# A 31-tap depthwise convolution as matrices of 4 time phases x 32 channels on TensorE

## The chip, the cores and the metric

The kernel runs on one core of a Trainium2 chip. The metric is the device time of one execution in microseconds (us); lower is better. A core has TensorE (matrix products, written to PSUM), VectorE, ScalarE (activations and casts), GpSimd and SyncE, whose only work here is to issue DMAs. In the lines of the profile they are PE (PEld for its weight loads), DVE, ACT, POOL and SP. "L165" is line 165 of the kernel file.

## What is computed

A trunk of four layers over 512 tokens of 1024 channels in float32. Each layer has a token mixer and then a gated conv-FFN, both behind an RMS norm and with a residual sum. The mixers are, in order: conv module, neighbourhood attention, retention, conv module. The change is inside the conv module, which so runs twice, as the first and the fourth mixer:

```python
def dwconv(x, w, b):
    k, c = w.shape
    y = lax.conv_general_dilated(
        x, w[:, None, :].astype(x.dtype), window_strides=(1,),
        padding=[(k // 2, k // 2)], dimension_numbers=('NWC', 'WIO', 'NWC'),
        feature_group_count=c)
    return y + b

def conv_module(h, w_in, b_in, dw_w, dw_b, ln_g, ln_b, w_out):
    a, gt = jnp.split(h @ w_in + b_in, 2, axis=-1)
    u = a * jax.nn.sigmoid(gt)
    u = dwconv(u, dw_w, dw_b)
    u = layernorm(u, ln_g, ln_b)
    return jax.nn.silu(u) @ w_out
```

`dw_w` has 31 taps per channel, so every output of the depthwise convolution is a weighted sum of 31 neighbouring tokens of its own channel.

## The kernel before

**Layout and arithmetic.** Activations lie channel-major: a tile is 128 channels (partitions) by 512 tokens, and `x` is eight such tiles. Matrix products run in the format `F32R`. To keep float32 accuracy each operand is split into a high part (a cast to `F32R` on ScalarE) and a low part (the difference, on VectorE), and `mm3` issues three matmuls per product: high x high, high x low, low x high. Weights come as tiles of 128 x 1024 on SyncE's DMA queue (`load_raw`, L150) and are split by `split_w` (L159 on ScalarE, L160 on VectorE). `split` (L174, L175) does the same for activations. The lines of `mm3` are L164 to L166.

**Order.** The program is written with a scheduler that orders the instructions of each engine from their order in the source, their readiness in its own model of time, and free buffers. On the chip every engine then runs its queue in that fixed order and waits for what is missing. `tc.issue_after` adds an order by hand. A pool with `bufs=n` has n buffers for a name; a tile that finds none free waits for the oldest to be read.

**The conv stage, `conv`.** It walks over m = 0..7, the groups of 128 channels.

- `front(m)`: the in-projection of value and gate, 2 x 24 matmuls of 512 columns into two PSUM banks; the norm's factor is applied afterwards (L341, L343), sigmoid on ScalarE (L342), the product is `u` (L345), padded by 15 zeros on either side. Then `u` is split into `uh`, `ul`, and the first taps run on TensorE: per tap a 128 x 128 diagonal matrix of the tap's weights, high and low, multiplied with `u` shifted by the tap, into bank `A`. How many taps go there stands in `TAPS`: the first number of each triple, for each layer and group. The diagonal matrices are built by `diag`, on GpSimd (L370) or ScalarE (L375).
- `taps(m, u, A)`, called two groups later (`LT`): the second number of taps goes as a product on ScalarE (L387, L391) and a sum on GpSimd (L392, into `pacc`); the others go on VectorE, partly into `A` (L406), partly into the tile `c8[m]` (L398, L402, L409). L411 and L412 add the three.
- `lnstat(m)`, two groups after that (`LS`): four transposes on TensorE (L420) and statistics per token on VectorE (L422), because the layer norm runs over channels.
- After the loop the statistics are combined, mean and `rstd` are spread over partitions by transposes (`bcast`, L200), and per group VectorE subtracts and multiplies (L460, L463), ScalarE applies Silu and the cast (L464, L466) and VectorE makes the low part (L469). Then eight outputs of the out-projection, 24 matmuls each, are added to `x` (`residual`, L244) and handed on to the next stage's `prep`.

For the first layer the weights of group 0 are loaded and split ahead, in the program's last part, together with `x`.

Of the kernel before, what the change touches and what calls it, by code (L numbers as in the profile page):

```python
# [8 lines left out]
F32 = mybir.dt.float32  # L9
# [8 lines left out]
P = 128  # L18
T = 512
# [14 lines left out]
for _name, _w in (  # L34
    ("n1g", 32), ("n2g", 32), ("cbin", 32), ("cdw", 2 * 8 * CW), ("cdb", 16),
    ("clg", 16), ("clb", 16), ("qg", 1), ("kg", 1), ("gng", 16), ("logd", 8),
    ("fdw", 4 * 44 * FC), ("fdb", 4 * 44),
):
    COLS[_name] = _n
    _n += _w  # L40
# [8 lines left out]
ID = True  # L49
# [7 lines left out]
NDB = 3  # L57
NPB = 0
NU = 3
NPR = 4  # L60
LT = 2
LS = 2
DH = ("PPPAPPPP", "PPPPPPPP")
DL = ("AAAAAAAP", "AAAAPAAP")
# [13 lines left out]
def tile_trunk(  # L78
# [3 lines left out]
    cw_in, cw_out, nat_qkv, rpb, nat_out,  # L82
# [220 lines left out]
    def conv(j, after):  # L303
        PAD = CW // 2
        TW = T + 2 * PAD
        dw0 = COLS["cdw"] + j * 8 * CW
        with ExitStack() as st:
            stage_pools(st, 9, 4, 4)
            cp = st.enter_context(tc.tile_pool(name=nm("cv"), bufs=1, reuse_waits=RW))
            c8 = [cp.tile([P, T], F32, tag=f"c{i}", name=nm("c")) for i in range(8)]  # L310
            bst = cp.tile([P, 4, 8, 6], F32, tag="bst", name=nm("bst"))
            dwh = cp.tile([P, 8 * CW], F32R, tag="dwh", name=nm("dwh"))
            dwl = cp.tile([P, 8 * CW], F32, tag="dwl", name=nm("dwl"))
            with ExitStack() as s2:
                up = s2.enter_context(tc.tile_pool(name=nm("cvu"), bufs=1, reuse_waits=RW))
                dp = s2.enter_context(tc.tile_pool(name=nm("cvd"), bufs=2, reuse_waits=RW))
                rp = s2.enter_context(tc.tile_pool(name=nm("cvr"), bufs=NPR, reuse_waits=RW))
                us = [up.tile([P, TW], F32, tag=f"u{i}", name=nm("u")) for i in range(NU)]
                for u in us:
                    nc.vector.memset(u[:, :PAD], 0.0)  # L320
                    nc.vector.memset(u[:, PAD + T:], 0.0)
                def front(m):
# [9 lines left out]
                    else:  # L332
                        for (ps, c) in ((pa, m), (pg, m + 8)):
                            wh, wl = load_w(cw_in[j, c], D)
                            for k in range(KD):
                                s = slice(k * P, (k + 1) * P)
                                mm3(ps, wh[:, s], wl[:, s], xhi[k], xlo[k], k == 0, k == KD - 1)
                            if m == 0:
                                stats1() if c == 0 else stats2()
# [8 lines left out]
                    npe = TAPS[j][m][0]  # L348
                    if ID and m not in diags:
                        with tc.issue_after(state["sqlast"].ins):  # L350
                            diags[m] = diag(m)
                    dh, dl = diags.pop(m) if m in diags else diag(m)
                    uh = dp.tile([P, TW], F32R, tag="uh", name=nm("uh"))
                    ul = dp.tile([P, TW], F32R, tag="ul", name=nm("ul"))
                    split(u, uh, ul)
                    for i in range(npe):
                        mm3(A, dh[:, i, :], dl[:, i, :], uh[:, i:i + T], ul[:, i:i + T],
                            i == 0, i == npe - 1)
                    return m, u, A

                diags = {}

                def diag(m):
                    npe = TAPS[j][m][0]
                    dh = dp.tile([P, npe, P], F32R, tag="dh" if m < 7 else "dh7", name=nm("dh"), bufs=NDB if m < 7 else 1)
                    dl = dp.tile([P, npe, P], F32R, tag="dl" if m < 7 else "dl7", name=nm("dl"), bufs=NDB if m < 7 else 1)
                    idb = ident.unsqueeze(1).broadcast_to([P, npe, P])
                    for dst, src, eng in ((dh, dwh.bitcast(F32), DH[j][m]), (dl, dwl, DL[j][m])):
                        if eng == "P":
                            nc.gpsimd.tensor_tensor(  # L370
                                dst, idb,
                                src[:, m * CW:m * CW + npe].unsqueeze(2).broadcast_to([P, npe, P]), MUL)
                        else:
                            for i in range(npe):
                                nc.scalar.activation(dst[:, i, :], ident, AF.Copy,  # L375
                                                     scale=src[:, m * CW + i:m * CW + i + 1])
                    return dh, dl

                def taps(m, u, A):
                    npe, npool, na = TAPS[j][m]  # L380

                    def wt(tap):
                        c = dw0 + m * CW + tap
                        return pt[:, c:c + 1]

                    pacc = dp.tile([P, T], F32, tag="pacc", name=nm("pacc"))
                    nc.scalar.activation(pacc, u[:, npe:npe + T], AF.Identity,  # L387
                                         bias=pc("cdb", j * 8 + m), scale=wt(npe))
                    for tap in range(npe + 1, npe + npool):
                        pr = rp.tile([P, T], F32, tag="pr", name=nm("pr"))  # L390
                        nc.scalar.activation(pr, u[:, tap:tap + T], AF.Copy, scale=wt(tap))  # L391
                        nc.gpsimd.tensor_tensor(pacc, pacc, pr, ADD)  # L392
                    ta = list(range(npe + npool, npe + npool + na))
                    tb = list(range(npe + npool + na, CW))
                    B = c8[m]
                    if tb:
                        t = tb.pop(0)
                        nc.vector.tensor_scalar(B, u[:, t:t + T], wt(t), None, MUL)  # L398
                    lead = max(0, len(tb) - len(ta))
                    for n in range(lead):  # L400
                        t = tb.pop(0)
                        nc.vector.scalar_tensor_tensor(B, u[:, t:t + T], wt(t), B, MUL, ADD)  # L402
                    while ta or tb:
                        if ta:
                            t = ta.pop(0)
                            nc.vector.scalar_tensor_tensor(A, u[:, t:t + T], wt(t), A, MUL, ADD)  # L406
                        if tb:
                            t = tb.pop(0)
                            nc.vector.scalar_tensor_tensor(B, u[:, t:t + T], wt(t), B, MUL, ADD)  # L409
                    if npe + npool + na < CW:  # L410
# [5 lines left out]
                def lnstat(m):  # L416
# [4 lines left out]
                    for b in range(4):  # L421
                        nc.vector.bn_stats(bst[:, b, m, :], tp[:, b * P:(b + 1) * P])  # L422
# [654 lines left out]
```

## Time and profile before

| | us |
|---|---|
| median of 3 runs | 2710.16 |
| lowest and highest run | 2708.76, 2711.47 |
| profiled execution, span | 2709.2 |
| busy in it: TensorE | 2583.4 |
| VectorE | 1824.4 |
| ScalarE | 1115.2 |
| GpSimd | 493.6 |

The span runs from the first to the last instruction of one profiled execution; engines work side by side, so the busy times don't add up to it. The DMAs moved 232.01 MB. The first conv stage fills the first 269 us of the span, the fourth mixer lies between about 2077 and 2335 us. Most of the rest is in-projections, FFNs and attention on TensorE.

A group line of the profile gives line, engine, operation, output and inputs, shape and count; then the busy time of the group in us and the mean of one in ns; then the engine's idle time ahead of it and what ended it. A timeline line gives start and duration in us. A line of waits gives who waited for whom, the total in us, how often, and the longest. Where matmuls overlap, their durations are longer than the distance of their starts.

### The profile page before, as it was taken

What the parts mean: (1) busy time and instruction counts of PE and PEld (TensorE: products, weight loads), DVE (VectorE), ACT (ScalarE), POOL (GpSimd) and SP (SyncE); (2) the same over time, 40 slices, a digit from 0 to 9 for tenths busy, and PEclk for the clock granted to TensorE, in tenths of its full rate; (3) what the DMA queues carried; (4) which work ended last, traced back from release to release, by engine and by line L of the source; (5) the groups of instructions that cost most, each with busy time, mean ns of one, the idle gap of its engine ahead of it and who ended that gap; (6) DMA issues with size and microseconds to landing.
All of it is one profiled execution on the core that took longest, in us unless ns stands there. A gap on an engine that the chain in (4) does not pass through costs nothing.

```text
span 2709.2 us, 31043 instructions
## 1 busy us (share of the span) xinstructions
PE 2583.4 (95%) x12018; PEld 2108.1 (78%) x12018; DVE 1824.4 (67%) x2742; ACT 1115.2 (41%) x1628; POOL 493.6 (18%) x337
## 2 busy tenths in 40 slices
PE   7878999999999999999999999999999776999999
PEld 5656888889998788888888888788887664888887
DVE  8997677535888777734656466777634999677732
ACT  6544444333655444423333323444423544444421
POOL 5873000002432100000000000100002874200000
PEclk9888999999999999999999999999999897999999
DMA  3111422333333222233222221222232110322232
GB/s 119 47 39 55 146 93 94 95 94 105 98 93 93 78 94 94 90 93 112 78 86 70 86 76 64 87 94 94 92 98 89 48 39 23 102 94 93 93 104 84
DMA packets 72995, 232.01 MB, mean 86 GB/s; under 512 B 11920, under 2 KB 16144, under 8 KB 72848
## 3 DMA queue, kind: packets, MB, share of 16 engines
q1 hardware_dynamic: 71488, 225.48, 26.2%
q0 software_dynamic: 640, 3.15, 0.5%
q8 instruction: 94, 1.54, 0.2%
q10 hardware_dynamic: 720, 1.41, 0.2%
q14 instruction: 53, 0.43, 0.1%
HBM read 224.50 MB, written 5.63 MB: 85 GB/s over the span
## 4 chain that ended last, share of the span: by engine, by line
PE 83%; DVE 15%; issue 1%; ACT 1%; DMA 0%; SPq 0%; ACTq 0%; DVEq 0%
PE ps L165 25%; PE ps L164 25%; PE ps L166 24%; DVE c L402 4%; PE ps L170 3%; PE ps L171 3%; PE ps L169 3%; DVE c L409 2%; DVE wl L160 2%; DVE ps L406 1%; DVE c L411 1%; DVE u L345 1%; DVE xl L214 1%; DVE ul L175 1%; DVE bst L422 0%
## 5 line engine op out<-in xcount | busy, mean ns | idle before, releaser
L159 ACT CAST wh<-wr 128x1024 fp32r<-128x1024 f32 (+1 forms) x414 | 427.1, 1032 | 1049.7 <-PE ps L165 789.6
L165 PE MATMUL ps<-xl,wh 128*128 128x512 f32 x1920 | 768.6, 400 | 4.3 <-DVE xl L214 4.3
L164 PE MATMUL ps<-xh,wh 128*128 128x512 f32 x1920 | 762.5, 398 | 8.8 <-ACT xh L213 6.7
L166 PE MATMUL ps<-xh,wl 128*128 128x512 f32 x1920 | 761.9, 397 | 3.6 <-DVE wl L160 3.6
L160 DVE TENSOR_TENSOR wl<-wr,wh 128x1024 fp32r<-128x1024 f32 (+1 forms) x410 | 514.2, 1255 | 341.8 <-ACT wh L159 339.3
L164 PEld LDWEIGHTS ps<-xh,wh 128*128 128x128 f32 x1920 | 363.8, 189 | 101.3 <-ACT xh L213 7.7
L165 PEld LDWEIGHTS ps<-xl,wh 128*128 128x128 f32 x1920 | 363.8, 189 | 92.3 <-DVE xl L214 6.6
L166 PEld LDWEIGHTS ps<-xh,wl 128*128 128x128 f32 x1920 | 363.8, 189 | 90.6 <-DVE wl L160 4.4
L222 POOL TENSOR_TENSOR sqacc<-t,sqacc 128x512 f32<-128x512 f32 x49 | 78.8, 1608 | 1188.4 <-ACT t L220 1168.6
L166 PE MATMUL ps<-hh,wl 128*128 128x512 f32 x704 | 278.0, 395 | 0.0
L164 PE MATMUL ps<-hh,wh 128*128 128x512 f32 x704 | 278.0, 395 | 0.0
L165 PE MATMUL ps<-hl,wh 128*128 128x512 f32 x704 | 278.0, 395 | 0.0
L392 POOL TENSOR_TENSOR pacc<-pacc,pr 128x512 f32<-128x512 f32 x155 | 255.3, 1657 | 77.0 <-ACT pr L391 58.9
L268 DVE TENSOR_TENSOR t<-ps,rstd_bc 128x512 f32<-128x512 f32 x176 | 120.9, 691 | 157.6 <-PE ps L166 157.3
L244 DVE TENSOR_TENSOR x<-ps,x 128x512 f32<-128x512 f32 x80 | 54.7, 690 | 170.3 <-PE ps L166 170.3
L170 PE MATMUL ps<-wl,xh 128*128 128x256 f32 (+1 forms) x512 | 159.2, 312 | 0.6 <-DVE wl L160 0.6
L171 PE MATMUL ps<-wh,xl 128*128 128x256 f32 (+1 forms) x512 | 159.1, 312 | 0.0
L169 PE MATMUL ps<-wh,xh 128*128 128x256 f32 (+1 forms) x512 | 158.5, 312 | 0.0
L166 PEld LDWEIGHTS ps<-hh,wl 128*128 128x128 f32 x704 | 132.3, 188 | 31.9
L165 PEld LDWEIGHTS ps<-hl,wh 128*128 128x128 f32 x704 | 132.3, 188 | 31.8
L164 PEld LDWEIGHTS ps<-hh,wh 128*128 128x128 f32 x704 | 132.3, 188 | 31.7
L271 ACT ACTIVATE t<-t,par 128x512 f32<-128x512 f32 x176 | 142.7, 815 | 11.8 <-DVE t L268 11.7
(222 smaller groups left out, 3609.8 us busy)
## 6 DMA issues: line engine op xcount, KB each, us to landing
wr<-in_f_up SPq DMA_DIRECT2D x176, 512.0 KB, 3.5
wr<-in_f_down SPq DMA_DIRECT2D x64, 448.0 KB, 3.4
wr<-in_f_down SPq DMA_DIRECT2D x32, 512.0 KB, 3.5
wr<-in_cw_in SPq DMA_DIRECT2D x30, 512.0 KB, 3.4
wr<-in_nat_qkv SPq DMA_DIRECT2D x24, 512.0 KB, 3.6
wr<-in_cw_out SPq DMA_DIRECT2D x16, 512.0 KB, 3.4
wr<-in_ret_qk SPq DMA_DIRECT2D x16, 512.0 KB, 3.4
wr<-in_ret_v SPq DMA_DIRECT2D x16, 512.0 KB, 3.4
```

The costliest lines, as they stand in the source:

```text
L159: nc.scalar.copy(hi[:, :n], raw[:, :n])
L160: eng.tensor_tensor(lo[:, :n], raw[:, :n], hi[:, :n].bitcast(F32), SUB)
L164: nc.tensor.matmul(o, wh, ah, start=first, stop=False)
L165: nc.tensor.matmul(o, wh, al, start=False, stop=False)
L166: nc.tensor.matmul(o, wl, ah, start=False, stop=last)
L169: nc.tensor.matmul(o, ah, wh, start=first, stop=False)
L170: nc.tensor.matmul(o, ah, wl, start=False, stop=False)
L171: nc.tensor.matmul(o, al, wh, start=False, stop=last)
L268: nc.vector.tensor_tensor(u, ps, rstd_bc, MUL)
L271: nc.scalar.activation(a, u, AF.Identity, bias=pc("fdb", l * 44 + c), scale=pt[:, w + 1:w + 2])
L392: nc.gpsimd.tensor_tensor(pacc, pacc, pr, ADD)
L402: nc.vector.scalar_tensor_tensor(B, u[:, t:t + T], wt(t), B, MUL, ADD)
```

## The change

All 31 taps run on TensorE, without diagonal matrices. The time axis is cut into four phases (token = 4q + s, `SH` = 4) and the channels into blocks of 32, so a contraction over 128 partitions holds 4 phases x 32 channels. For each block of 32 channels a matrix of 128 x 128 maps the four input phases to the four output phases at one shift of q, and nine shifts (`NA`) cover the 31 taps. The host prepares these matrices (`cdw`): 32 blocks per layer, each 128 x 1152 float32, 0.590 MB.

- `front(m)` computes the gate before the value, writes `u` phase by phase with four zeros at either end of each (`QL` = 136), splits it into `hl`, writes `hl` to DRAM with one DMA from GpSimd's queue and reads it back with four, rearranged to `X`: partitions 4 phases x 32 channels, for four blocks.
- `taps(m, X)`, two groups later (`LAG`): per block the raw matrices are loaded on SyncE's queue and split. For each of nine shifts `X` is the stationary operand: one matmul of 256 columns (X high by the matrix's high and low) and one of 128 columns (X low by the high part). The result comes out token-major: partition q, columns phase and channel. Two VectorE instructions of 256 columns per half group add the products, the bias and write it to `y`.
- The layer norm's statistics are then along the free axis (three `bn_stats` per phase); mean and `rstd` are per-partition scalars. `norm(k)` normalises four pieces of 128 columns, transposes them back to channel-major on TensorE, and ScalarE applies Silu; then the split as before.
- The out-projection's first two outputs advance together with `norm`, chunk by chunk. Tokens are in the order phase, q, so the residual sum (`finish`) reads PSUM and writes `x` through a rearranged view.
- The vector and GpSimd taps, the diagonal matrices, `lnstat` and the broadcasts of mean and `rstd` are gone. The bias of the convolution is loaded as a tile of 128 x 1024 (0.524 MB) on ScalarE's queue at the start of each conv stage.

```diff
-ID = True
...
-TAPS = (
-    ((6, 11, 5), (4, 11, 2), (7, 14, 2), (5, 11, 5), (9, 12, 1), (8, 9, 3), (11, 11, 4), (14, 8, 3)),
-    ((6, 10, 5), (5, 9, 0), (7, 14, 3), (5, 11, 5), (11, 11, 1), (8, 9, 3), (10, 12, 4), (14, 8, 3)),
-)
...
+QL = 136
+SH = 4
+NA = 9
+LAG = 2
...
+            dram = st.enter_context(tc.tile_pool(name=nm("cvx"), bufs=3, space=bass.MemoryType.DRAM))
+            y = cp.tile([P, SH, D], F32, tag="y", name=nm("y"))
+            bias = cp.tile([P, D], F32, tag="bias", name=nm("bias"))
+            nc.scalar.dma_start(bias, cdb[j])
+            bst = cp.tile([P, SH, 3, 6], F32, tag="bst", name=nm("bst"))
...
-                        for (ps, c) in ((pa, m), (pg, m + 8)):
+                        for (ps, c) in ((pg, m + 8), (pa, m)):
...
-                    u = us[m % NU]
+                    u = us[m % 2]
                     nc.vector.scalar_tensor_tensor(
-                        u[:, PAD:PAD + T], ta, pc("cbin", j * 16 + m), tg, ADD, MUL)
-                    A = bank(psb)
...
+                        u[:, :, 4:4 + P], ta.rearrange("p (q s) -> p s q", s=SH),
+                        pc("cbin", j * 16 + m), tg.rearrange("p (q s) -> p s q", s=SH), ADD, MUL)
+                    hl = dp.tile([P, SH, 2, QL], F32R, tag="hl", name=nm("hl"))
+                    split(u, hl[:, :, 0, :], hl[:, :, 1, :])
+                    ud = dram.tile([P, 2 * SH * QL], F32R, tag="ud", name=nm("ud"))
+                    nc.gpsimd.dma_start(ud, hl.rearrange("p s h q -> p (s h q)"))
+                    X = dp.tile([P, 4, 2, QL], F32R, tag="X", name=nm("X"), bufs=3)
+                    uv = ud.rearrange("(b c) (s n) -> s c b n", b=4, s=SH)
+                    for s in range(SH):
+                        nc.gpsimd.dma_start(X[32 * s:32 * s + 32].rearrange("p b h q -> p b (h q)"), uv[s])
+                    return X
+
+                def taps(m, X):
+                    for half in range(2):
+                        ps = bank(psb)
+                        for i in range(2):
+                            b = half * 2 + i
+                            raw = dp.tile([P, NA, P], F32, tag="wraw", name=nm("wraw"), bufs=3)
+                            nc.sync.dma_start(raw.rearrange("p a n -> p (a n)"), cdw[j, m * 4 + b])
+                            W = dp.tile([P, NA, 2, P], F32R, tag="W", name=nm("W"), bufs=3)
+                            split(raw, W[:, :, 0, :], W[:, :, 1, :])
+                            o = ps[:, i * 256:(i + 1) * 256]
+                            for a in range(NA):
+                                nc.tensor.matmul(o, X[:, b, 0, a:a + P],
+                                                 W[:, a].rearrange("p h n -> p (h n)"),
+                                                 start=a == 0, stop=False)
+                                nc.tensor.matmul(o[:, :P], X[:, b, 1, a:a + P], W[:, a, 0, :],
+                                                 start=False, stop=a == NA - 1)
+                        c0 = m * P + half * 64
+                        pv = ps.rearrange("p (b h r c) -> p h r b c", b=2, h=2, r=SH)
+                        t = t512()[:, :256].rearrange("p (r b c) -> p r b c", r=SH, b=2)
+                        bb = bias[:, c0:c0 + 64].rearrange("p (b c) -> p b c", b=2)
+                        nc.vector.tensor_tensor(
+                            t, pv[:, 1], bb.unsqueeze(1).broadcast_to([P, SH, 2, 32]), ADD)
+                        yv = y[:, :, c0:c0 + 64].rearrange("p r (b c) -> p r b c", b=2)
+                        nc.vector.tensor_tensor(yv, pv[:, 0], t, ADD)
+                    for n, (k0, k1) in enumerate(((0, 4), (4, 7), (7, 8))):
+                        if m == k1 - 1:
+                            for r in range(SH):
+                                nc.vector.bn_stats(bst[:, r, n, :], y[:, r, k0 * P:k1 * P])
+
                 fr = {}
-                for m in range(8 + LT + LS):
+                for m in range(8 + LAG):
                     if m < 8:
                         fr[m] = front(m)
...
+                    if m >= LAG:
+                        taps(m - LAG, fr.pop(m - LAG))
...
+            def norm(k):
+                c = slice(k * P, (k + 1) * P)
+                tp = bank(psb)
+                for r in range(SH):
+                    nc.vector.tensor_scalar(y[:, r, c], y[:, r, c], mv[:, 2 * r:2 * r + 1],
+                                            rs[:, r:r + 1], SUB, MUL)
+                    nc.tensor.transpose(tp[:, r * P:(r + 1) * P], y[:, r, c], ident)
+                t = t512()
+                nc.scalar.activation(t, tp, AF.Silu, bias=pc("clb", j * 8 + k),
+                                     scale=pc("clg", j * 8 + k))
+                split(t, sh[k], sl[k])
...
+            def finish(o, ps):
+                xv = x[o].rearrange("p (q r) -> p r q", r=SH)
+                nc.vector.tensor_tensor(xv, ps.rearrange("p (r q) -> p r q", r=SH), xv, ADD)
+                after(o)
+
+            w0, w1 = load_w(cw_out[j, 0], D), load_w(cw_out[j, 1], D)
+            p0, p1 = bank(psa), bank(psa)
+            norm(0)
             for k in range(8):
...
+                if k < 7:
+                    norm(k + 1)
+                out_mm(p0, w0, k)
+                out_mm(p1, w1, k)
+            finish(0, p0)
+            finish(1, p1)
+            for o in range(2, 8):
...
```

More of the change, by code (lines that the diff above doesn't have):

```diff
@@ L316, in conv @@
                 dp = s2.enter_context(tc.tile_pool(name=nm("cvd"), bufs=2, reuse_waits=RW))
-                rp = s2.enter_context(tc.tile_pool(name=nm("cvr"), bufs=NPR, reuse_waits=RW))
-                us = [up.tile([P, TW], F32, tag=f"u{i}", name=nm("u")) for i in range(NU)]
+                us = [up.tile([P, SH, QL], F32, tag=f"u{i}", name=nm("u")) for i in range(2)]
                 for u in us:
-                    nc.vector.memset(u[:, :PAD], 0.0)
-                    nc.vector.memset(u[:, PAD + T:], 0.0)
+                    nc.vector.memset(u[:, :, :4], 0.0)
+                    nc.vector.memset(u[:, :, QL - 4:], 0.0)
                 def front(m):
@@ L352, in front @@
[L352 to L410, printed above, removed]
-                        nc.vector.tensor_tensor(B, B, pacc, ADD)
-                        nc.vector.tensor_tensor(B, A, B, ADD)
-                    else:
-                        nc.vector.tensor_tensor(B, A, pacc, ADD)
@@ L416, in lnstat @@
-                def lnstat(m):
-                    tp = bank(psb)
-                    for b in range(4):
-                        s = slice(b * P, (b + 1) * P)
-                        nc.tensor.transpose(tp[:, s], c8[m][:, s], ident)
-                    for b in range(4):
-                        nc.vector.bn_stats(bst[:, b, m, :], tp[:, b * P:(b + 1) * P])
-                split(pt[:, dw0:dw0 + 8 * CW], dwh, dwl)
-                for m in range(min(NPB, 8)):
-                    diags[m] = diag(m)
+                        u[:, :, 4:4 + P], ta.rearrange("p (q s) -> p s q", s=SH),
@@ L427, in conv @@
                 fr = {}
-                for m in range(8 + LT + LS):
+                for m in range(8 + LAG):
                     if m < 8:
                         fr[m] = front(m)
-                    if 0 <= m - LT < 8:
-                        taps(*fr[m - LT])
-                    if 0 <= m - LT - LS < 8:
-                        lnstat(m - LT - LS)
+                    if m >= LAG:
+                        taps(m - LAG, fr.pop(m - LAG))
             mv = sm(8)
-            for b in range(4):
-                nc.vector.bn_aggr(mv[:, 2 * b:2 * b + 2], bst[:, b])
@@ new lines, in out_mm @@
+            def out_mm(ps, w, k):
+                s = slice(k * P, (k + 1) * P)
+                mm3(ps, w[0][:, s], w[1][:, s], sh[k], sl[k], k == 0, k == 7)
+            def finish(o, ps):
[5 more added lines that the diff above has]
+            norm(0)
@@ L486, in conv @@
-                residual(o, ps)
-                after(o)
+                    out_mm(ps, w, k)
+                finish(o, ps)
     def nat(after):
@@ L1032, in _layout @@
     rel = (np.arange(DTAB)[None, :] - 384 - np.arange(P)[:, None]).astype(np.float32)
+    cdw = np.zeros((2, 32, SH, 32, NA, SH, 32), np.float32)
+    taps = f["conv_dw_w"].reshape(2, CW, 32, 32)
+    ci = np.arange(32)
+    for sh in range(SH):
+        for r in range(SH):
+            for a in range(NA):
+                tap = SH * a + sh - r - 1
+                if 0 <= tap < CW:
+                    cdw[:, :, sh, ci, a, r, ci] = taps[:, tap]
     qkv = f["nat_w_qkv"][0].reshape(2, 4, P, 3, 4, 256).transpose(3, 4, 0, 2, 1, 5)
```

73 lines of the change are left out of this document (11 added, 62 removed).

## The prediction

> **What bounds the kernel now.** I read the page from the top: busy shares, then the slices, then the same stretches as windows, then the waits of the two convolution stages.
>
> ```profile
> span 2709.2 us, 31043 instructions
> PE 2583.4 (95%) x12018; PEld 2108.1 (78%) x12018; DVE 1824.4 (67%) x2742; ACT 1115.2 (41%) x1628; POOL 493.6 (18%) x337
> PE   7878999999999999999999999999999776999999
> ```
>
> TensorE is busy 95% of the span, but not evenly: the low digits stand in the first four slices and again near slice 32, where the two conv layers are. The windows name what is busy there instead, and show the granted clock.
>
> ```profile
> core 0: us, PE busy (x) PEld busy (x) DVE busy (x) ACT busy (x) POOL busy (x), PEclk, DMA share, GB/s
> 0.00:130.00 130.00, 100.50 (x374) 77.73 (x375) 121.27 (x129) 79.08 (x147) 89.49 (x54) 0.89 0.25 83
> 130.00:206.00 76.00, 57.69 (x227) 44.76 (x226) 76.00 (x89) 35.72 (x53) 57.04 (x37) 0.85 0.13 42
> 2065.00:2260.00 195.00, 154.28 (x620) 120.00 (x619) 178.08 (x183) 94.53 (x158) 138.05 (x79) 0.92 0.16 54
> ```
>
> In both layers VectorE is busy over 90% and GpSimd about 70%, while TensorE is idle a fifth to a quarter of the time, at a clock of 0.85 to 0.92. So the conv stage is bound by the taps on VectorE and GpSimd. What TensorE waits for, first layer (0 to 275 us) and then second (2077 to 2336):
>
> ```profile
> PE ps L165 <- DVE ul L175: 16.6, 6, 5.1
> PE ps L164 <- ACT uh L174: 14.4, 3, 7.7
> ...
> PE ps L164 <- ACT uh L174: 23.8, 5, 6.9
> PE ps L165 <- DVE ul L175: 13.1, 7, 5.2
> ```
>
> 31.0 and 36.9 us: the tap matmuls stand on TensorE right behind the in-projection of the same channels and wait for gate and split, which queue behind vector taps. Everywhere else TensorE has hardly a gap, so the time saved or lost is that of the two conv stages, counted on TensorE.
>
> **Prices on TensorE.**
>
> ```profile
> 2077.54 0.39 PE L164 MATMUL ps<-xh,wh 128*128 128x512 f32 x1
> ...
> 2084.54 0.40 PE L166 MATMUL ps<-xh,wl 128*128 128x512 f32 x1
> ```
>
> These are 31 dense matmuls of 512 columns (thirty steps, 7.00 us): 0.233 us each. The durations overlap, so the price is the step between starts. In-projection: 384 x 0.233 = 89.6 us per layer; out-projection: 192 x 0.233 = 44.8. Taps removed: 64 in the first layer and 66 in the second on TensorE (sums of the first numbers in TAPS), three matmuls each: 44.8 and 46.2 us.
>
> Added: 32 blocks per layer of 9 pairs, one matmul 256 wide (X high by the matrix's high and low) and one 128 wide (X low by high), each with its own 128-column weight load.
>
> ```profile
> 693.05 0.28 PE L170 MATMUL ps<-wl,xh 128*128 128x256 f32 x1
> 693.16 0.22 PE L164 MATMUL ps<-ph,va 128*64 128x128 f32 x1
> ...
> 693.82 0.22 PE L166 MATMUL ps<-ph,vs 128*64 128x128 f32 x1
> 693.88 0.33 PE L171 MATMUL ps<-wh,xl 128*128 128x256 f32 x1
> 694.05 0.28 PE L169 MATMUL ps<-wh,xh 128*128 128x256 f32 x1
> L169 PEld LDWEIGHTS ps<-wh,xh 128*128 128x128 f32 x512 | 96.0, 188 | 5.8
> L166 PEld LDWEIGHTS ps<-ph,va 128*64 128x64 f32 x64 | 8.6, 135 | 0.0
> ```
>
> A 256-wide matmul steps by 0.11 to 0.12. A 128-wide one steps by 0.06 when its weights have 64 columns: from 693.16 to 693.82 are 11 steps in 0.66 us. When the matmul behind it needs 128 columns, as in the new code, the two steps from 693.82 to 694.05 take 0.23 instead of 0.18: the load does not fit behind so short a matmul. The weight-load rows say the same, 188 - 135 = 53 ns for 64 more columns, so some 106 for 128. A pair is therefore **0.23 us**; lower end 0.118 + 0.059 = 0.177. For the upper end neither load hides at all: 2 x 0.188 = 0.38. I take 0.23, its own row: 288 x 0.23 = 66.2 us per layer, 2.07 per block (51.0 to 109).
>
> The Trainium skill ("TensorE: Matmul & The Clock Gate", Back-to-back issue gap) gives sustained load-and-matmul steps of about 81 ns at 128 columns and 131 at 512. With 81 for the short matmul the taps would take 57 us and the result would be some 18 us lower. The trace has 0.233 where the page has 131 ns, so the row stands.
>
> **What the other engines get.** Per group of 128 channels TensorE now needs 48 x 0.233 + 4 x 2.07 = 19.5 us.
>
> ```profile
> L160 DVE TENSOR_TENSOR wl<-wr,wh 128x1024 fp32r<-128x1024 f32 x346 | 444.3, 1285 | 240.2 <-ACT wh L159 239.6
> L175 DVE TENSOR_TENSOR ol<-ps,oh 64x256 fp32r<-64x256 f32 x32 | 13.2, 412 | 4.4 <-ACT oh L174 3.8
> L159 ACT CAST wh<-wr 128x1024 fp32r<-128x1024 f32 x350 | 366.7, 1048 | 814.0 <-PE ps L165 554.0 <-issue 179.6 <-PE ps L171 51.0
> L847 DVE TENSOR_SCALAR o<-ps,mv,sm 128x512 f32<-128x512 f32 x16 | 12.8, 802 | 0.1
> L631 DVE TENSOR_SCALAR e<-e,sm 128x256 f32<-128x256 f32 x64 | 31.5, 529 | 0.3
> wr<-in_cw_in SPq DMA_DIRECT2D x30, 512.0 KB, 3.4
> vs<-va POOLq DMA_DIRECT2D x8, 384.0 KB, 5.4
> q1 hardware_dynamic: 71488, 225.48, 26.2%
> q0 software_dynamic: 640, 3.15, 0.5%
> 730.44 0.57 POOL L561 DMA_DIRECT2D vs<-va  x1 [8.88 <-DVE va L175]
> ```
>
> VectorE loses all its taps. It gains four matrix splits of 1152 columns (1.285 x 1152/1024 = 1.45 each, 5.8) and four evictions of 256 columns from PSUM (0.41 each, 1.6); it keeps two weight splits (2.6) and the gate with its split (about 3.2, estimated as five passes of 512 columns at half of 1.285). Sum 13.2 of 19.5 us. ScalarE: four casts of 1.18, two of 1.05 and some 1.4 for sigmoid and split (an estimate, two 512-column passes somewhat above half of 1.05), 8.2 us. GpSimd only issues DMAs. So TensorE becomes the bound, and these costs are hidden; without that cover VectorE's 13.2 would stand first.
>
> DMA per group: two weight tiles of 0.524 MB, four matrices of 0.590 MB, and 0.557 MB written to DRAM and read back, 4.52 MB. By the queue rows 225.48 MB took 26.2% of the span (318 GB/s at full use) and software DMAs about 233 GB/s: 10.7 + 4.8 = 15.5 us of 19.5. Hidden, but with little room. SP's queue is in order: a matrix load that waits for its buffer holds the weight tiles behind it, and TensorE waits for those. I put 4 us per layer for late matrices, between nothing and the third rival.
>
> The round trip of X: gate and split some 3.6 us (the same five passes, in a row with ScalarE's), write 5.4, three further issues of 0.57 and a read of 5.4: 16 us. LAG = 2 covers it by two groups in mid-stage. After the last in-projection only taps 5 and 6 cover it, 2 x 8.3 = 16.6 us, with loaded queues: 3 us per layer. The reads wait on GpSimd's queue behind the write's landing; nothing else is queued there in this stage. Going by the Trainium skill ("DMA: Bandwidth & Descriptors", Anatomy of one DMA), 2.0 us plus bytes over 436 GB/s, a leg takes 3.3 us and these 3 us vanish; the 5.4 row, for fewer bytes, speaks for the longer leg.
>
> **The end of the stage and the out-projection.** The first layer's wait for its last chunks, and matmuls at the seams of both:
>
> ```profile
> PE ps L420 <- DVE c L412: 4.9, 2, 4.2
> 206.87 0.41 PE L166 MATMUL ps<-uh,dl 128*128 128x512 f32 x1
> 222.40 0.79 PE L164 MATMUL ps<-sh,wh 128*128 128x512 f32 x1 [2.28 <-ACT sh L466]
> 268.43 0.39 PE L166 MATMUL ps<-sh,wl 128*128 128x512 f32 x1
> 2334.26 0.39 PE L166 MATMUL ps<-sh,wl 128*128 128x512 f32 x1
> 18.93 0.39 PE L166 MATMUL ps<-xh,wl 128*128 128x512 f32 x1
> ```
>
> Last tap to first out-matmul takes 15.1 us now (207.3 to 222.4). Of it 4.9 are the wait for the vector taps of the last chunks (L412), which go. Aggregates, root, Silu and split stay; the two broadcasts by transposes go, while two evictions, four normalisations and four transposes come in ahead of Silu. I take these as equal: 15.1 - 4.9 = 10.2, say 10.3 us, the same in both layers. TensorE is idle meanwhile as it is now, so the slow clock afterwards stays too.
>
> Out-projection now: 46.4 us for 44.8 of work, 1.6 for that clock. The new order normalises chunk by chunk with two outputs behind it. Two tensor-scalar rows (802 ns for 512 columns, 529 for 256) give 0.26 us fixed and 0.53 per 512, so 0.40 for 128: VectorE needs 4 x 0.40 + 0.64 = 2.24 us per chunk, TensorE 6 x 0.233 = 1.4. Over eight chunks that is up to 6.7 us; a third and fourth output can fill it, down to nothing. I take 3, so 44.8 + 1.6 + 3 = 49.4.
>
> **The sum.** First layer: the in-projection of group 0 is done at about 19.2 (its pace is ScalarE's and the DMA's). The 0.5 MB bias load now runs beside the start, 0.524/318 = 1.6 us at most; I take 1.0. Then 7 x 11.2 = 78.4, eight transposes for the norm's statistics 0.9 (at 0.11), taps 66.2, late matrices and X 7, seam 10.3, out 49.4: end at 232.4 against 268.8, **-36.4 us**. Second layer: 2077.5 + 89.6 + 0.9 + 66.2 + 7 + 10.3 + 49.4 = 2300.9 against 2334.7, **-33.8**. The FFNs behind start alike. Span 2709.2 - 70.2 = 2639.0. The median of the three runs, 2710.16, is 0.96 above the profiled span: **2640 us**.
>
> **The rivals.** (1) The pair is cheap and nothing stalls: 0.177 saves 30.4 and the 7 us drop out twice: 2640 - 30 - 14 = 2596. For it: records of 0.06 steps; against: the 0.23 row with 128-column weights. (2) The old stall comes back in another shape: TensorE's queue is in order, and W and X, like uh and ul, come over several engines. If 25 of the present 31 to 37 us of waits return in each layer above my 7, it is 2690. For it: those waits; against: LAG, and VectorE at 13.2 of 19.5. (3) **Slower**: the DMAs can't carry it. Place: matrices and X in the tap stage. It decides once the transfers of a group take 24.4 us (the 19.5, the 0.5 already allowed and the 35.1/8 of gain), which is 185 GB/s. At 180 GB/s a group takes 25.1 us, (25.1 - 19.5) x 8 - 4 = 40.8 more per layer: 2722. For it: the needed 232 GB/s stands in no slice of this page,
>
> ```profile
> GB/s 119 47 39 55 146 93 94 95 94 105 98 93 93 78 94 94 90 93 112 78 86 70 86 76 64 87 94 94 92 98 89 48 39 23 102 94 93 93 104 84
> ```
>
> the highest is 146. Against: the same queue's 318 GB/s of engine time, and half a megabyte landing in 3.4 us with several loads in flight. (4) TensorE wasn't kept from anything and the added 20 us per layer of taps just replaces idle time with work: no change. The waits speak against it.
>
> **How the numbers follow.** Chances: forecast 0.58, (1) 0.12, (2) 0.20, (3) 0.08, (4) 0.02. The range goes from just above (1) to (2), 2600 to 2690, leaving out most of (1) and all of (3). This kernel's runs differ by 0.1%, so 0.2% is what a measurement can tell from no change; forecast, (1) and (2) are faster by more: 0.90, 0.02, 0.08.
>
> **What would show it.** Right: TensorE near 95% in both tap stages at clock 1.0, pairs stepping by 0.23, VectorE at two thirds, out-matmuls starting 10 us after the last tap, the first layer ending near 232. Wrong: pairs near 0.18 or above 0.3; TensorE waiting for W's split or for X's read; DMA share near 1; the seam not shorter than 15 us.

## The result and the profile after

| | us | ratio to before (95% interval) |
|---|---|---|
| before, median of 4 runs | 2710.75 | |
| changed kernel, median of 4 runs (2637.28 to 2643.66) | 2639.8 | 0.974 (0.9726 to 0.9754) |
| forecast | 2640.0, range 2600 to 2690 | |

The page of the changed kernel: busy time per engine, then rows in 40 slices.

```profile
span 2635.5 us, 32343 instructions
PE 2595.6 (98%) x12764; PEld 2151.0 (82%) x12764; DVE 1649.0 (63%) x2627; ACT 1047.9 (40%) x1423; POOL 233.6 (9%) x244
PE   8989999999999999999999999999999998999999
GB/s 267 232 139 134 112 92 93 95 95 108 92 95 77 90 95 96 92 95 108 80 80 72 87 74 70 82 96 89 94 95 99 248 238 103 98 89 95 94 107 79
```

TensorE is busy 12 us more than before and the span is 74 us shorter: the work grew, the gaps went. The low digits of the conv stages are gone, and the DMA rate there has tripled. Stretches of the first layer (after the start, middle of the taps, their end, the out-projection) and of the second (middle and end of the taps), as windows:

```profile
core 0: us, PE busy (x) PEld busy (x) DVE busy (x) ACT busy (x) POOL busy (x), PEclk, DMA share, GB/s
25.00:60.00 35.00, 35.00 (x168) 29.02 (x168) 19.66 (x32) 13.79 (x16) 8.30 (x15) 0.95 0.84 224
60.00:145.00 85.00, 85.00 (x526) 75.62 (x526) 57.17 (x68) 35.25 (x37) 10.83 (x20) 1.00 0.88 243
145.00:176.00 31.00, 27.47 (x217) 26.78 (x215) 21.17 (x28) 13.28 (x12) 2.71 (x5) 0.94 0.65 172
184.00:234.00 50.00, 49.77 (x219) 39.73 (x219) 32.19 (x49) 25.61 (x36) 11.77 (x7) 0.99 0.22 75
2060.00:2175.00 115.00, 115.00 (x684) 100.90 (x682) 74.56 (x87) 48.47 (x51) 19.05 (x35) 1.00 0.85 231
2175.00:2204.00 29.00, 26.32 (x210) 25.73 (x209) 20.32 (x28) 12.39 (x12) 2.71 (x5) 0.94 0.58 180
```

In mid-stage TensorE never stops, at a granted clock of 1.00, and VectorE is busy 67%. After the waits at the start and at the end of the taps the clock is 0.95 and 0.94. What is left are its waits, first stage (0 to 236 us; who waited for whom, total us, times, longest) and then the second (2042 to 2262):

```profile
PE ps L154 <- ACT xh L203: 6.5, 1, 6.5
PE ps L397 <- DVE y L395: 5.3, 1, 5.3
PE ps L357 <- DVE W L165: 3.4, 3, 1.5
PE ps L156 <- DVE wl L150: 1.4, 1, 1.4
PE ps L154 <- ACT wh L149: 0.5, 1, 0.5
...
PE ps L397 <- DVE y L395: 5.2, 1, 5.2
PE ps L357 <- DVE W L165: 2.6, 3, 1.6
```

L357 and L360 are the tap matmuls (256 and 128 columns), L397 the transposes of `norm`, L154 to L156 `mm3`. The first stage has lost the 31 us of waits for `uh` and `ul`, and no wait of that size has come in their place.

Timeline rows of TensorE, from just after the waits at the start, the middle of the taps and the seams of both layers:

```profile
25.13 0.63 PE L154 MATMUL ps<-xh,wh 128*128 128x512 f32 x1
25.56 0.63 PE L155 MATMUL ps<-xl,wh 128*128 128x512 f32 x1
...
86.73 0.33 PE L357 MATMUL ps<-W,X 128*128 128x256 f32 x1
86.90 0.22 PE L360 MATMUL ps<-W,X 128*128 128x128 f32 x1
86.96 0.33 PE L357 MATMUL ps<-W,X 128*128 128x256 f32 x1
...
175.70 0.22 PE L360 MATMUL ps<-W,X 128*128 128x128 f32 x1
183.92 0.80 PE L154 MATMUL ps<-sh,wh 128*128 128x512 f32 x1
232.81 0.40 PE L156 MATMUL ps<-sh,wl 128*128 128x512 f32 x1
...
2042.22 0.40 PE L154 MATMUL ps<-xh,wh 128*128 128x512 f32 x1
2203.72 0.22 PE L360 MATMUL ps<-W,X 128*128 128x128 f32 x1
2211.77 0.79 PE L154 MATMUL ps<-sh,wh 128*128 128x512 f32 x1
2260.65 0.39 PE L156 MATMUL ps<-sh,wl 128*128 128x512 f32 x1
```

A pair takes 0.23 us (86.73 to 86.96). The last out-matmul of the first layer starts at 232.81 instead of 268.43, 35.6 us earlier. The second layer lasts from 2042.22 to 2260.65, 218.4 us, where it took 256.7 (2077.54 to 2334.26): 38.3 us. Together 73.9, the whole difference of the spans (73.7).

### The profile page after: what moved, and what is told of

It reads as the page before. It is cut to its first block, busy times and chain, and to the rows that moved or that the text cites. A ratio compares the mean times of both kernels' runs of the same rounds, so it can differ in the third digit from the quotient of the medians.

```text
span 2635.5 us, 32343 instructions
## 1 busy us (share of the span) xinstructions
PE 2595.6 (98%) x12764; PEld 2151.0 (82%) x12764; DVE 1649.0 (63%) x2627; ACT 1047.9 (40%) x1423; POOL 233.6 (9%) x244
## 5 line engine op out<-in xcount | busy, mean ns | idle before, releaser
L154 PE MATMUL ps<-xh,wh 128*128 128x512 f32 x1920 | 760.3, 397 | 10.3 <-ACT xh L203 7.7
L156 PE MATMUL ps<-xh,wl 128*128 128x512 f32 x1920 | 758.8, 395 | 1.6 <-DVE wl L150 1.6
L150 DVE TENSOR_TENSOR wl<-wr,wh 128x1024 fp32r<-128x1024 f32 (+1 forms) x410 | 498.1, 1215 | 352.6 <-ACT wh L149 350.0
L154 PEld LDWEIGHTS ps<-xh,wh 128*128 128x128 f32 x1920 | 361.9, 188 | 101.6 <-ACT xh L203 8.5
L156 PEld LDWEIGHTS ps<-xh,wl 128*128 128x128 f32 x1920 | 361.9, 189 | 88.2 <-DVE wl L150 2.5
L156 PE MATMUL ps<-hh,wl 128*128 128x512 f32 x704 | 278.0, 395 | 0.0
L154 PE MATMUL ps<-hh,wh 128*128 128x512 f32 x704 | 278.0, 395 | 0.0
L154 PEld LDWEIGHTS ps<-hh,wh 128*128 128x128 f32 x704 | 132.3, 188 | 31.8
L156 PEld LDWEIGHTS ps<-hh,wl 128*128 128x128 f32 x704 | 132.3, 188 | 31.8
L357 PE MATMUL ps<-W,X 128*128 128x256 f32 x576 | 138.2, 337 | 6.1 <-DVE W L165 6.1
L265 DVE SCALAR_TENSOR_TENSOR t<-t,par,t 128x511 f32<-128x511 f32 x176 | 131.9, 750 | 5.6
```

The costliest lines, as they stand in the source:

```text
L150: eng.tensor_tensor(lo[:, :n], raw[:, :n], hi[:, :n].bitcast(F32), SUB)
L154: nc.tensor.matmul(o, wh, ah, start=first, stop=False)
L156: nc.tensor.matmul(o, wl, ah, start=False, stop=last)
L265: nc.vector.scalar_tensor_tensor(a[:, :T - 1], u[:, 1:], pt[:, w + 2:w + 3], a[:, :T - 1], MUL, ADD)
L357: nc.tensor.matmul(o, X[:, b, 0, a:a + P], W[:, a].rearrange("p h n -> p (h n)"), start=a == 0, stop=False)
```

## The experiments

Each edit is to the changed kernel unless it says otherwise. All times are medians beside runs of the kernel before on the same chip, which gave 2709.4 to 2710.9. The runs of the changed kernel itself spread from 2637.3 to 2643.7, so two or three microseconds from its 2639.8 tell nothing.

**What bounded the kernel before: order or load?** The kernel before, with its tap matmuls issued two groups later:

```diff
-                    A = bank(psb)
...
-                    for i in range(npe):
-                        mm3(A, dh[:, i, :], dl[:, i, :], uh[:, i:i + T], ul[:, i:i + T],
-                            i == 0, i == npe - 1)
-                    return m, u, A
+                    return m, u, dh, dl, uh, ul
...
-                def taps(m, u, A):
+                def taps(m, u, dh, dl, uh, ul):
                     npe, npool, na = TAPS[j][m]
+                    A = bank(psb)
+                    for i in range(npe):
+                        mm3(A, dh[:, i, :], dl[:, i, :], uh[:, i:i + T], ul[:, i:i + T],
+                            i == 0, i == npe - 1)
```

> The kernel before, with its tap matmuls moved from behind the in-projection of their own group to the place of the other taps, two groups later (three buffers for uh and ul). All work stays. TensorE waited 31.0 and 36.9 us for uh and ul there. Rival: the order alone made those waits, and any version with two groups between gets them back: 60 us less, 2650. Theory: TensorE waited because VectorE, slowed by GpSimd, is the bound: VectorE is busy 197 of the first 206 us and 178 of 195 in the second stage, so whatever the order, at most 9 and 17 us can go: 2685 to 2710.

Measured: 2711.5, ratio 1.0007 (0.9997 to 1.0017). Nothing went. Its waits of TensorE in the first stage, and VectorE in the same stretch as before:

```profile
PE ps L419 <- DVE c L411: 18.4, 4, 9.9
PE ps L166 <- DVE wl L160: 13.2, 2, 10.6
PE ps L165 <- DVE ul L175: 9.7, 2, 6.9
...
130.00:206.00 76.00, 53.70 (x211) 41.81 (x210) 76.00 (x86) 35.11 (x58) 57.02 (x35) 0.84 0.12 40
```

VectorE is again busy for all of the 76 us. The wait only changed its name: from `uh` and `ul` to the finished chunks (18.4) and weights (13.2), everything that VectorE makes. So moving the matmuls was not what gained: with VectorE as full as before, the order is worth nothing. The reader may note how little "who waited for whom" says by itself: the name at the wait is the next thing late on a saturated engine.

**Was GpSimd what made VectorE slow?** The kernel before without GpSimd's taps:

```diff
-                    for tap in range(npe + 1, npe + npool):
-                        pr = rp.tile([P, T], F32, tag="pr", name=nm("pr"))
-                        nc.scalar.activation(pr, u[:, tap:tap + T], AF.Copy, scale=wt(tap))
-                        nc.gpsimd.tensor_tensor(pacc, pacc, pr, ADD)
```

> The kernel before, without the taps on GpSimd: the products on ScalarE (L391) and the sums on GpSimd (L392) are left out, some ten taps of 31 are missing from the convolution. Taps on VectorE and TensorE stay. Theory: the conv stage was bound by VectorE, and VectorE was slowed by GpSimd working beside it: a 512-column vector tap took 1345 ns on average in the conv stages, the same form 745 ns in the FFNs. Without GpSimd's sums the taps fall to 0.75 us, VectorE's work falls by some 56 us per layer (124 us of taps, u and low parts in the first layer to 69), TensorE becomes the bound, and each layer loses 40 to 55 us: 2600 to 2630. Rival: the long durations are VectorE's own and GpSimd is not their cause: above 2690.

Measured: 2606.8, 103 us less than before. The vector taps, grouped by line: the kernel before in its first 206 us (tap on an SBUF tile; tap accumulated in PSUM), then this run over both layers (the same two):

```profile
L402 DVE SCALAR_TENSOR_TENSOR c<-u,par,c 128x512 f32<-128x512 f32 x39 | 50.5, 1313 | 0.0
L406 DVE SCALAR_TENSOR_TENSOR ps<-u,par,ps 128x512 f32<-128x512 f32 x22 | 16.4, 743 | 0.0
```

```profile
L397 DVE SCALAR_TENSOR_TENSOR c<-u,par,c 128x512 f32<-128x512 f32 x81 | 64.4, 813 | 0.0
...
L401 DVE SCALAR_TENSOR_TENSOR ps<-u,par,ps 128x512 f32<-128x512 f32 x49 | 36.3, 744 | 12.2 <-PE ps L166 12.2
```

The tap with both tensors in SBUF falls from 1313 to 813 ns; the tap that accumulates in PSUM takes 743 either way. The edit also takes ScalarE's products away, but the trace of the kernel before tells the two apart: of its 81 instructions of L402, 16 ran while GpSimd stood still, and they took 735 to 752 ns, 8 of them with ScalarE busy beside them for over nine tenths of the time; the 48 beside which GpSimd was busy that much took 1587 on average. So the old split of the taps paid twice: GpSimd's ten taps took its own time and slowed VectorE's. How the 103 us divide between the two, this run doesn't say. The Trainium skill ("SBUF — State Buffer", Who interferes with whom) says that a VectorE instruction with two SBUF inputs contends with a GpSimd instruction that reads SBUF, and that one with at most one SBUF input does not, outside VectorE's two-port modes; the rows of the two taps agree with it.

**The price of a pair.** The short matmul widened from 128 to 256 columns:

```diff
-                                nc.tensor.matmul(o[:, :P], X[:, b, 1, a:a + P], W[:, a, 0, :],
-                                                 start=False, stop=a == NA - 1)
+                                nc.tensor.matmul(o, X[:, b, 1, a:a + P],
+                                                 W[:, a].rearrange("p h n -> p (h n)"),
+                                                 start=False, stop=a == NA - 1)
```

> The short matmul (X low by the high part, 128 columns) also multiplies the low part and so becomes 256 wide; the output then holds one more product than the changed kernel's. Theory: what a pair of matmuls costs is set by the weight load that has to fit behind the short one (about 0.11 us), not by its 128 columns. Widening it to a step of 0.118 then takes a pair from 0.23 to 0.236 us: 288 x 0.005 per layer, some 3 us in all, 2643. Rival: the columns set the price. Then a pair grows by 0.059 us, 17 us per layer, and the time is 2674.

Measured: 2637.7 (2636.9 to 2639.3), no difference from 2639.8. Timeline of this run:

```profile
86.92 0.28 PE L357 MATMUL ps<-W,X 128*128 128x256 f32 x1
87.04 0.28 PE L360 MATMUL ps<-W,X 128*128 128x256 f32 x1
87.16 0.28 PE L357 MATMUL ps<-W,X 128*128 128x256 f32 x1
```

A pair now takes 0.24 us with 512 columns where it took 0.23 with 384. A third more columns cost nothing that can be measured. Together with the rows at 693 us, where 128-wide matmuls with 64 weight columns step by 0.06, this says that the load of 128 weight columns was the price of the short matmul. Its step is 0.23 - 0.117 = 0.11 us. The Trainium skill ("TensorE: Matmul & The Clock Gate", LDWEIGHTS) gives a load as its columns over 1.2 in ns; 107 ns for 128 columns is an estimate from it, and the step agrees.

**How near are the DMAs?** Two runs. In the first the short matmul is left out:

```diff
-                                                 start=a == 0, stop=False)
-                                nc.tensor.matmul(o[:, :P], X[:, b, 1, a:a + P], W[:, a, 0, :],
-                                                 start=False, stop=a == NA - 1)
+                                                 start=a == 0, stop=a == NA - 1)
```

> The short matmul is left out (the product X low by high is missing from the output), one 256-wide matmul per shift remains: 0.118 instead of 0.23 us. If TensorE alone bounds the tap stage, each layer loses 288 x 0.114 = 33 us: 2574. Theory: TensorE is the bound, but the DMAs stand close behind it. Their share is 0.85 to 0.88 of the 19.5 us of a group, 17 us, so a group can't get shorter than about 17 and a layer gains only (19.5 - 17) x 8 = 20 us: about 2600, with TensorE waiting for loads in mid-stage.

In the second every matrix is loaded twice:

```diff
                             nc.sync.dma_start(raw.rearrange("p a n -> p (a n)"), cdw[j, m * 4 + b])
+                            raw2 = dp.tile([P, NA, P], F32, tag="wraw2", name=nm("wraw2"), bufs=2)
+                            nc.sync.dma_start(raw2.rearrange("p a n -> p (a n)"), cdw[1 - j, m * 4 + b])
...
+                            nc.scalar.copy(raw2[:, 0, :1], raw2[:, 0, 1:2])
```

> Each matrix load is followed by a second one of the same size into a tile that nothing uses (ScalarE touches one column to free it). It prices the rival that forecast a slower kernel. Theory: a group then needs 17.0 us of DMA as measured plus 2.36 MB / 318 GB/s = 7.4, 24.4 us against 19.5 of TensorE: 4.9 x 8 = 39 us per layer, 2718, DMA share near 1 in the tap stages. Rival: the measured DMA share overstates how full the engines are and the transfers still hide: below 2660.

Measured: 2593.5 and 2658.9. The first tap stage as windows, first with one matmul (to the last in-projection, and behind it), then with double loads (the middle):

```profile
30.00:128.00 98.00, 98.00 (x520) 83.23 (x519) 75.00 (x90) 50.29 (x53) 17.59 (x33) 1.00 0.96 271
128.00:155.00 27.00, 17.55 (x91) 15.79 (x90) 19.60 (x27) 11.11 (x11) 4.26 (x8) 0.75 0.78 215
```

```profile
60.00:145.00 85.00, 85.00 (x540) 76.11 (x539) 55.12 (x65) 36.92 (x52) 11.15 (x21) 1.00 1.09 355
```

The last row settles it. With 355 GB/s instead of 243 TensorE still stands for no moment of the 85 us. The theory, 39 us more per layer, falls; 19 us came in all, and the part that shows as waits lies at the start and the end of the stage. A DMA share of 0.88 was no sign that only a tenth of room was left. The first run gave about the forecast time, 46 us less instead of 66, but not for the reason given. Its waits in the first stage:

```profile
PE ps L357 <- DVE W L165: 3.3, 4, 1.6
PE ps L357 <- DMA X<-ud: 2.8, 1, 2.8
PE ps L357 <- DVE t L364: 2.7, 1, 2.7
```

8.8 us against 3.4 in the changed kernel, and all of them between 130 and 151 us, behind the last in-projection (its last matmul starts at 125.56). In mid-stage, where an in-projection stands between two groups of taps, TensorE never stops, the clock is 1.00, and a group takes 15.6 us (the taps of two groups start at 79.14 and 94.75): shorter than the 17 that the theory held for the least. The loss is at the end, where groups of taps follow each other: TensorE is busy for 17.55 of 27 us, at a clock of 0.75. There a group needs 36 x 0.117 = 4.2 us of TensorE, but by the rows of the changed kernel VectorE's four splits (1.36 each) and four evictions (0.42) need some 7.1, and its matrices 2.36 MB. In the second layer matrices make 7.8 us of waits and X 1.1. Of the missing 20 us some 12 are waits and some 10 steps of TensorE that are longer than at full clock, counted over both layers of the two traces. Which of VectorE, the buffers and the loads would have to give way there was not tried. The Trainium skill ("DMA: Bandwidth & Descriptors", Where 436 GB/s comes from) puts the HBM limit of a core near 358 GB/s; 355 is below it, and no run here shows whether it is a limit.

**The end of the tap stage: matrices or X?** Five buffers for the raw matrices:

```diff
-                            raw = dp.tile([P, NA, P], F32, tag="wraw", name=nm("wraw"), bufs=3)
+                            raw = dp.tile([P, NA, P], F32, tag="wraw", name=nm("wraw"), bufs=5)
```

> Five buffers instead of three for the raw matrices. Theory: TensorE's waits for a matrix at the end of the tap stages (3.4 and 2.6 us) come from loads issued too late, since a load waits for one of three buffers and takes 6 us to land. With five they start earlier and the waits go: 6 us less, 2634. Rival: the DMA engines are simply busy there with other loads, and the same bytes land no earlier: 2640.

Measured: 2641.2 (2638.6 to 2642.5), no gain, yet not by the rival's way. Waits in the first and the second stage:

```profile
PE ps L357 <- DMA X<-ud: 3.7, 1, 3.7
PE ps L154 <- ACT wh L149: 3.3, 1, 3.3
...
PE ps L357 <- DMA X<-ud: 4.0, 1, 4.0
```

The waits for matrices are gone, as the theory said, and a wait for X has taken their place: two chains had been late by nearly the same time. At the start the wait for the in-projection's weights has grown from 0.5 to 3.3 us, with more matrix loads in flight ahead of them. To see X alone, LAG = 1:

```diff
-LAG = 2
+LAG = 1
```

> LAG = 1 instead of 2 in the changed kernel: the taps of a group come one group after its in-projection. Theory: the way of X from the last in-projection matmul to landing takes 18 us in the changed kernel's trace (145.2 to some 163). In mid-stage one tap group and one in-projection, 19.5 us, still cover it. At the end only one tap group of 8.3 us does, so TensorE waits some 9.7 us for X in place of the present 3.4 and 2.6 for matrices: 7 us per layer, 2653, and a wait on X of 8 to 10 us at the end of each tap stage. Rival A: X never stands on the path, no change. Rival B: the DMA queues are so loaded that every group waits, 16 waits of 2 us and more: above 2670.

Measured: 2649.7, 10 us more (expected 13). The trace is of the slowest of its four runs, 2654.1. Waits, first and second stage:

```profile
PE ps L357 <- DMA X<-ud: 10.7, 4, 6.5
...
PE ps L357 <- DMA X<-ud: 9.4, 3, 6.5
```

The wait of 6.5 us in each layer comes at the end: X stands on the path there, as the theory had it, with 6.5 instead of the 9.7 worked out. The other five, 0.8 to 1.9 us, come earlier, three of them in mid-stage (the first at 91 us): there the theory had X covered, and for these groups it wasn't quite. They are fewer and shorter than rival B had them.

**The start, and a version that is faster than both.** First the start alone:

```diff
-            nc.scalar.dma_start(bias, cdb[j])
...
-                    nc.scalar.activation(tg, tg, AF.Sigmoid, bias=pc("cbin", j * 16 + 8 + m))
+                    state["sg"] = nc.scalar.activation(tg, tg, AF.Sigmoid, bias=pc("cbin", j * 16 + 8 + m))
...
-                            split(raw, W[:, :, 0, :], W[:, :, 1, :])
+                            with tc.issue_after(state["sg0"].ins):
+                                split(raw, W[:, :, 0, :], W[:, :, 1, :])
...
+                    if m == 0:
+                        state["sg0"] = state["sg"]
+                        with tc.issue_after(state["sg0"].ins):
+                            nc.scalar.dma_start(bias, cdb[j])
```

> The changed kernel; the bias load and the splits of the first matrices are issued on ScalarE after the first group's sigmoid. Theory: the first layer starts late because the bias load runs beside the first loads (first matmul at 6.5 instead of 5.5 us) and because three matrix casts (3.25 us on ScalarE) go ahead of the weights of the second in-projection (TensorE waits 0.46 and 1.39 us). Both go: 2.8 us less, 2637, all of it before 35 us. Rival: the matrices then come late for the first tap group, and the time comes back there: 2640.

Measured: 2637.8 (2635.0 to 2640.0), not to be told from the changed kernel. Timeline rows of TensorE and, between them, of ScalarE:

```profile
5.54 0.80 PE L154 MATMUL ps<-xh,wh 128*128 128x512 f32 x1 [5.54 <-ACT xh L203]
...
19.77 1.05 ACT L149 CAST wh<-wr 128x1024 fp32r<-128x1024 f32 x1 [2.91 <-DMA wr<-in_cw_in]
...
23.86 0.50 PE L156 MATMUL ps<-xh,wl 128*128 128x512 f32 x1 [2.26 <-DVE wl L150]
```

Half of the theory holds: without the bias load the first matmul starts at 5.54 instead of 6.49. But the wait for the second in-projection's low part stays, 2.26 us instead of 1.4 + 0.5, so the three casts were not its cause, and the early microsecond is lost again by 24 us. The trace shows what makes that weight late: without the casts ScalarE is idle for 2.91 us, until 19.77, because the weights haven't landed (in the changed kernel it began the same cast at 19.60), and VectorE comes to the low part only at 22.58, behind the norm's statistics. After the wait TensorE is faster than in the changed kernel: the granted clock from 25 to 60 us is 1.00 instead of 0.95. In the two traces the first layer's last out-matmul starts at 230.22 instead of 232.81, but the second layer takes 221.8 us instead of 218.4, and the sum is nothing. Why the second was longer was not taken apart.

Then start, LAG and buffers together:

```diff
-LAG = 2
+LAG = 3
...
-                    X = dp.tile([P, 4, 2, QL], F32R, tag="X", name=nm("X"), bufs=3)
+                    X = dp.tile([P, 4, 2, QL], F32R, tag="X", name=nm("X"), bufs=4)
...
-                            raw = dp.tile([P, NA, P], F32, tag="wraw", name=nm("wraw"), bufs=3)
+                            raw = dp.tile([P, NA, P], F32, tag="wraw", name=nm("wraw"), bufs=4)
```

> The start as in the run before, and LAG = 3 with four buffers each for X and the raw matrices. In the run with five matrix buffers the waits for matrices went and a wait of 3.7 and 4.0 us for X took their place. With LAG = 3 three tap groups (25 us) follow the last in-projection and cover X's 18 us. Theory: both waits go, 3.4 and 2.6 us, and 2.8 at the start: 2631. Rival: another load is late instead (weights of the out-projection, or the third group's in-projection at the start): 2637 or more.

Measured: **2631.3** (2630.2 to 2632.5), ratio 0.9709 (0.9694 to 0.9723) to before, 8.5 us less than the changed kernel, as the theory said. Waits for matrices, first and second stage, with none for X:

```profile
PE ps L357 <- DVE W L165: 2.5, 3, 1.0
...
PE ps L357 <- DVE W L165: 1.5, 2, 1.0
```

The time came out, but not by the terms of the theory: the waits for matrices fell by 2.0 us in the two layers together, not by 6.0, and those at the start are 1.4, 1.2 and 0.5 us, where the theory had none. The two traces differ by 5.9 us, 4.6 of them in the two conv stages. Of these 0.9 is the earlier first matmul, 0.7 are fewer waits, and some 3 are steps of TensorE nearer to full clock (from 145 to 176 us the clock is 1.00 instead of 0.94). With five buffers alone nothing was gained, and with all of it 8.5 us; LAG = 3 alone was not run, so whether it takes both is not shown.

## Why the prediction was right

| step | forecast | measured |
|---|---|---|
| a pair of tap matmuls | 0.23 us | 0.23 |
| VectorE in a group of 19.5 us | 13.2 | 67% of it, 13.1 |
| bias load beside the start | 1.0 | 1.0 (6.49 and 5.54), and 1.9 of other waits |
| late matrices and X, per layer | 4 + 3 | 3.4 and 2.6, all matrices |
| seam, end of the last tap to first out-matmul | 10.3 | 8.0 and 7.8 (to 183.92, 2211.77) |
| out-projection | 49.4 | 49.3 (183.92 to 233.21) |
| gain of the first and second layer | 36.4, 33.8 | 35.6, 38.3 |

**The bound** was named rightly: the taps on VectorE and GpSimd. The two runs on the kernel before show it from both sides, with the order changed and nothing gained, and with GpSimd's taps left out and 103 us gained. That GpSimd makes VectorE's taps longer was not in the prediction; it came with the second of these runs. The forecast didn't need it, since both kinds of taps go.

**The price on TensorE** carried the sum, and it was right because it was read at a place where a 128-wide matmul stands ahead of a 128-column weight load. From the step of the other 128-wide matmuls, 0.06, the taps would have been priced 15 us per layer too low.

**Where the gain came from**, first layer: TensorE's tap work grew by 66.2 - 44.8 = 21.4 us. Its waits in that stage fell from 58.5 to 17.3 us (the sums of the two lists whose main rows are shown), 41.2, of which 31 are those for `uh` and `ul`. That leaves 35.6 - 41.2 + 21.4 = 16 us, and they go to the clock. In the first 206 us of before, 601 matmuls took 158.2 us of busy time (both windows together), where 0.233 each makes 140, and 28 of them are transposes that need less; the changed kernel's mid-stage runs at 1.00. Taking the steps of TensorE's matmuls one by one from both traces gives nearly the same: what they are longer than at full clock falls from 25.7 to 10.8 us in the first layer and from 18.3 to 5.7 in the second. This split is worked out from two profiles, not tried alone.

**Sizes that were off, and cancelled.** That 2640 met 2639.8 is in part luck: the first layer gained 0.8 us less than forecast and the second 4.5 more. The terms:

- The start lost 1.9 us of waits that the sum didn't have.
- The slower clock after a wait was in the sum for the seam alone. It also follows the waits at the start and at the end of the taps: clock 0.95 over 35 us, 0.94 over 31 and 0.94 over 29 are some 1.7 to 1.9 us each. The two rows from 25 us step by 0.43 instead of 0.233. It does not follow every wait: in the run with the start changed the clock stayed 1.00 after one of 2.26 us.
- The terms for matrices and for X were added, though both chains run beside each other and only the later one shows: 3.4 and 2.6 instead of 7.
- The seam was over 2 us shorter than by "I take these as equal".
- The out-projection came out by chance. The 3 us for VectorE's pace with the chunks did not come: TensorE stands for 0.2 us in that stretch. But 21 of the 32 transposes of `norm` run there, for which the sum had no term, and their steps make some 3.2 us.

The second layer has none of the first one's extra cost at the start, so its gain is the larger one.

**The rivals.** (1), cheap pairs: excluded by the step of 0.23. (2), the old waits in another shape: 3.4 and 2.6 us returned, not 25. (3), DMAs that can't carry it: the DMAs would have had to be held to 185 GB/s, and they moved 243 in the changed kernel and 355 in the run with double loads, with TensorE busy throughout. The prediction's own "little room", 15.5 of 19.5 us, was drawn from shares of the queues' engine time, and there was more room than that. (4) fell with the gain.

## What to carry to other kernels

When an engine is saturated, the waits in the profile name whatever it makes next; moving the waiting work renamed the wait here and gained nothing; unloading the engine did. Price a short matmul by the weight load behind it, at a place of the trace where that same pair stands: with 128 weight columns a 128-wide matmul cost as much as a 256-wide one. Where two chains end late at the same place, relieving one shows the other: change both before judging either. And compare a forecast term by term: a total can be met while its terms miss on both sides.

## What the runs showed of the hardware

- GpSimd's sums slowed vector instructions with both tensors in SBUF (1313 to 813 ns once they were out; 735 to 752 while GpSimd stood still), and not those that accumulate in PSUM (743 and 744).
- A DMA share near 0.9 left room for 46% more bytes (243 to 355 GB/s). At 355 GB/s the share was 1.09, so it is not a share of what the engines can do.
- After waits of 0.46 and 1.39 us at the start TensorE's 512-wide matmuls stepped by 0.43 instead of 0.233 us for 3 us (rows from 25.13).
- Vector instructions that walk an SBUF tile in steps of four elements were slower than their contiguous forms, as groups of the changed kernel show: residual sum with `x` in steps (L409) and without (L234), and `u` from tiles read in steps (L333).

```profile
L409 DVE TENSOR_TENSOR x<-ps,x 128x512 f32<-128x512 f32 x16 | 17.5, 1108 | 31.3 <-PE ps L156 31.3
L234 DVE TENSOR_TENSOR x<-ps,x 128x512 f32<-128x512 f32 x64 | 43.8, 690 | 145.7 <-PE ps L156 145.7
L333 DVE SCALAR_TENSOR_TENSOR u<-t,par,t 128x512 f32<-128x512 f32 x16 | 18.3, 1146 | 1.2
```

In the run without GpSimd's taps the contiguous form of the last one took 741 ns. The prediction had priced these as contiguous; VectorE had the room, so it cost nothing here. That the steps are the cause was not tried by itself.
